# Splitting the head-group results into operand pairs where they are made, instead of in front of the output projection

## The chip, the core and the metric

One core of a Trainium2 chip runs the kernel. The metric is device microseconds of one execution. Three runs of the kernel before gave 2999.87, 3000.15 and 3003.53 us; the median is 3000.15. The profile is of a further execution, which took 2992.77 us.

## What is computed

One decoder layer over 2048 tokens of width 1024, in fp32. The part that the change touches:

```
u = rmsnorm(h, attn_pre_norm)
hq, hf, hi, hg, sq, sk, sv = split(u @ w_in)
o_hg = hgrn2_mix(hq, hf, hi, lb)                       # gated linear recurrence, 4 heads of 128
o_hg = rmsnorm(o_hg, hg_out_norm) * silu(hg)
o_sb = stick_breaking_mix(sq, sk, sv)                  # causal attention, 8 heads of 64
o_sb = rmsnorm(o_sb, sb_out_norm)
mix  = concat(o_hg, o_sb) @ w_out
h    = h + rmsnorm(mix, attn_post_norm)                # then a SwiGLU FFN and a gated embedding
```

The two norms of the group results are by row, so the kernel multiplies the finished product rows by them; it only needs each group's sum of squares per row. The gain `hg_out_norm` is already in the gate; the gain `sb_out_norm` (`g_sb`) has to be put onto the attention result before the product.

## The kernel before

Every fp32 product is made of three fp32r matmuls (`mm3`, lines 215 to 217): each operand is a pair, `hi` (a rounded copy, written by ScalarE) and `lo` (the rest, written by VectorE or GpSimd). Tokens are worked in four groups of 512 (`g` = 0 to 3). A result tile has 128 partitions (columns of the model) by 512 tokens; a group has eight of them for the output projection, 0 to 3 from the recurrence, 4 to 7 from the attention (two heads of 64 in each).

The order of TensorE's instructions is the order in which the program is written: the function `weave` steps a main stream (an input projection, later an output projection) and takes steps of the attention and of the recurrence between its steps. On the other engines and on the DMA queue (SP) a scheduler chooses the order at build time. Every engine then works in order: an instruction that waits holds up all that stand behind it on its engine.

The attention is a chain of 320 units (a block of 128 queries against a chunk of 512 keys). Each unit makes scores (`z`, line 418), weights on ScalarE, VectorE and GpSimd (lines 424 to 443), and four units later transposes them (`turn_of`, `tr`, line 451) and multiplies them with the values (`values_of`, `av`, lines 467 and 468). When the last chunk of a head is done, lines 471 to 474 add the two halves of `av` (a ScalarE copy, a VectorE add) into a tile of 64 partitions, `avo`, and store it in DRAM (`o_s`). The last heads of the groups 0 to 3 end at 206, 462, 796 and 1334 us of the profile. The recurrence (`hgrn`) ends a head with lines 596 to 608: square, gate, store of `gate` to `o_s`; its sum of squares goes through a matmul with ones, line 613, after one further yield.

`out_load(g)` (line 619 on) reads the eight tiles of a group back through a tile `tmp` with two buffers. Of a recurrence tile it makes the pair with a ScalarE cast and a GpSimd subtraction (lines 201, 202); of an attention tile it makes the scaled pair (ScalarE line 629, VectorE line 630), and the square and its sum (ScalarE lines 634, 636, GpSimd line 637). The operands go to `uh` and `ul`, which have 16 pairs of buffers, shared with the operands of the input projection. It is called for group 0 before the last part of the input projection of group 3, and for the groups 1 to 3 before the output projections of the groups 0 to 2, a whole projection before the operands are used. `out_proj(g)` begins with `sums`: four matmuls of `acc` with ones (line 649), two VectorE copies, and two small GpSimd instructions that make the row scales `rg`.

Of the kernel before, what the change touches and what calls it, by code (L numbers as in the profile page):

```python
# [8 lines left out]
F32 = mybir.dt.float32  # L9
F32R = mybir.dt.float32r  # L10
# [80 lines left out]
def hybrid_block(  # L91
# [29 lines left out]
    h2t_s = scratch("h2t_s", (ND, P, GT))  # L121
    pt_s = scratch("pt_s", (PLE // P, P, GT))
    hid_s = [dram.tile([DFF // 256, 7, P, GT], F32, tag=f"hid_s{i}", name=f"hid_s{i}") for i in range(2)]
    o_s = [[dram.tile([P, GT], F32, tag=f"o_s{g}_{i}", name=f"o_s{g}_{i}") for i in range(ND)] for g in range(NG)]


    const = ctx.enter_context(tc.tile_pool(name="const", bufs=1))
# [3 lines left out]
    def ctile(name, shape, dt=F32, pool=const):  # L131
        return pool.tile(list(shape), dt, tag=name, name=name)
# [22 lines left out]
    oml = ctile("oml", (P, HH))  # L155

    masks = {h: ctile(f"mask{h}", (P, BL), U8, const1) for h in (0,) + LEVELS if h < BL}
    hgss = ctile("hgss", (P, NG, TT))


    ps = ctx.enter_context(tc.tile_pool(name="ps", bufs=1, space=bass.MemoryType.PSUM))
# [3 lines left out]
    def bank(tag):  # L165
        return ps.tile([P, 512], F32, tag=tag, name=tag, bufs=BANKS[tag])
# [12 lines left out]
    def ev(dt=F32, name="ev", shape=(P, GT)):  # L179
        return fb.tile(list(shape), dt, tag="ev", name=name, bufs=12)  # L180
# [98 lines left out]
    def operand(pool, tag, bufs):  # L279
        return [pool.tile([P, GT], F32R, tag=tag + s, name=tag + s, bufs=bufs) for s in ("h", "l")]  # L280

    def tmp(dt=F32):
        return wpool.tile([P, GT], dt, tag="tmp", name="tmp", bufs=2)


    def in_norm(g):
# [106 lines left out]
    def attention():  # L393
# [65 lines left out]
        def values_of(ch, sb, lo_c, hi, lo):  # L459
            st, c = ch["st"], ch["c"]  # L460
            g = st["g"]
            first = c == g and sb == 0
            last = c == 0 and sb == TT - 1
            if first:
                st["av"] = bank("av")
            av = st["av"]
            nc.tensor.matmul(av[:, lo_c:], ch["v"][:, sb, :], hi[:, lo_c:], start=first, stop=False)
            nc.tensor.matmul(av[:, lo_c:], ch["v"][:, sb, :], lo[:, lo_c:], start=False, stop=last)
            if last:
                h = st["h"]  # L470
                o = att.tile([SBD, GT], F32, tag="avo", name="avo", bufs=1)
                nc.scalar.copy(o, av[SBD:P, :])
                nc.vector.tensor_tensor(o, av[0:SBD, :], o, op=ALU.add)
                nc.sync.dma_start(o_s[g][HH + h // 2][(h % 2) * SBD:(h % 2 + 1) * SBD, :], o)

        units, turned = [], []
        chunks = [(g, h, c) for g in range(NG) for h in range(SBH) for c in range(g, -1, -1)]
        n_units = len(chunks) * TT
# [22 lines left out]
    def hgrn(g):  # L501
        acc = None
        for h in range(HH):
# [100 lines left out]
                nc.scalar.activation(q.rearrange(flat), ob, AF.Square)  # L604
                nc.gpsimd.tensor_tensor(acc, acc, q, op=ALU.add)
            nc.vector.tensor_tensor(gate.rearrange(flat), ob, gate.rearrange(flat), op=ALU.mult)
            nc.sync.dma_start(o_s[g][h], gate.rearrange(flat))
            nc.gpsimd.tensor_copy(hstate[h], s_last)
            yield
        yield  # L610
        b = bank("hg")
        for c in range(TT):
            nc.tensor.matmul(b[:, c:c + 1], acc[:, c, :], ones1, start=True, stop=True)
        nc.scalar.copy(hgss[:, g, :], b[:, 0:TT])
        yield

    HG_STEPS = HH * 11 + 2


    def out_load(g, res):  # L620
        ops = []
        acc = None
        for i in range(ND):
            raw = tmp()
            nc.sync.dma_start(raw, o_s[g][i])
            if i >= HH:
                hi, lo = operand(wpool, "u", UB)
                gs = g_sb[:, i - HH:i - HH + 1]
                nc.scalar.activation(hi, raw, AF.Copy, scale=gs)
                nc.vector.scalar_tensor_tensor(lo, raw, gs, hi.bitcast(F32), op0=ALU.mult, op1=ALU.subtract)  # L630
                ops.append((hi, lo))
                if i == HH:
                    acc = ev(name="oss")
                    nc.scalar.activation(acc, raw, AF.Square)
                else:
                    nc.scalar.activation(raw, raw, AF.Square)
                    nc.gpsimd.tensor_tensor(acc, acc, raw, op=ALU.add)
            else:
                ops.append(split(wpool, "u", UB, raw))
        res["o"], res["oss"] = ops, acc  # L640

    def out_proj(g, res):
        ops, acc = res["o"], res["oss"]
        r_hg, r_sb = [], []

        def sums(acc):
            b = bank("tr")
            for t in range(TT):
                nc.tensor.matmul(b[:, t:t + 1], acc[:, t * P:(t + 1) * P], ones1, start=True, stop=True)
            rr = const.tile([P, 2 * TT], F32, tag="rg", name="rg", bufs=2)  # L650
            nc.vector.tensor_copy(rr[:, 0:TT], hgss[:, g, :])
            nc.vector.tensor_copy(rr[:, TT:], b[:, 0:TT])
            nc.gpsimd.tensor_scalar(rr, rr, 1.0 / (HH * P), EPS, op0=ALU.mult, op1=ALU.add)
            nc.gpsimd.tensor_tensor(rr, rr, neghalf.to_broadcast((P, 2 * TT)), op=ALU.pow)
            r_hg.extend(rr[:, t:t + 1] for t in range(TT))
            r_sb.extend(rr[:, TT + t:TT + t + 1] for t in range(TT))

        sums(acc)
        mix = [[None, None] for _ in range(TT)]
        for quarter in range(4):  # L660
            half, o = divmod(quarter, 2)
# [708 lines left out]
```

## Time and profile before

| | us |
|---|---|
| median of three runs | 3000.15 |
| profiled execution | 2992.77 |
| its span, first to last instruction | 2990.8 |
| TensorE busy | 2901.4 |
| VectorE busy | 2071.8 |
| ScalarE busy | 1581.7 |
| GpSimd busy | 1398.8 |
| instructions on `tmp`, first start to last end | 918 to 1359, in four sets |

In the views, PE is TensorE, DVE is VectorE, ACT is ScalarE, POOL is GpSimd. A row of the timeline gives start, duration, engine, line, operation, output and input tile, and in brackets how long the engine had been idle and what ended that. A row of the waits gives who waited for whom, the sum in us, how often, and the longest. A row of the windows gives, for a stretch of the span, its length, the busy time of the engines, the granted TensorE clock as a share, and the DMA share and rate.

The sets of `tmp` lie at 918 to 951 (group 0), 1112 to 1151 (group 1), 1214 to 1245 (group 2) and 1320 to 1359 (group 3).

### The profile page before, as it was taken

Reading aid. Unit: us, or ns where it says so; the run is one execution under the profiler, and the core shown is the slowest. Engines: PE = TensorE matmul, PEld = TensorE weight load, DVE = VectorE, ACT = ScalarE, POOL = GpSimd, SP = SyncE. Lnnn points to the kernel's source line nnn. Section 1 sums busy time; section 2 is a strip of 40 time slices with the busy share of each in tenths; the row PEclk is TensorE's granted clock in tenths of the full one; section 3 lists DMA queues with packets and bytes.
Section 4 is the critical chain, followed back from the end, with each engine's and each line's share of the span. In section 5 each row is a group of like instructions: output and inputs, shape, how many; then the busy total and the mean of one; then the engine's idle time right before and its main releaser. Section 6 shows DMA issues by size and latency. Waiting matters only on the chain.

```text
span 2990.8 us, 52665 instructions
## 1 busy us (share of the span) xinstructions
PE 2901.4 (97%) x18188; PEld 2421.3 (81%) x18188; DVE 2071.8 (69%) x2993; ACT 1581.7 (53%) x3182; POOL 1398.8 (47%) x1396
## 2 busy tenths in 40 slices
PE   8999999999999999898999999999999999999999
PEld 7888788878787888788777788888788888878777
DVE  3566667787777776766888777565877765656785
ACT  5666756676667666777523334455433323545542
POOL 3344455555556665865622211355622121456653
PEclk9999999999999999899999999999999999999999
DMA  7775665455445444458877777666965555677974
GB/s 225 210 221 157 182 186 164 141 176 165 145 140 159 144 133 137 160 193 271 278 231 244 246 254 258 196 210 208 344 198 164 164 176 176 208 219 232 327 250 161
DMA packets 469418, 602.26 MB, mean 201 GB/s; under 512 B 43168, under 2 KB 277664, under 8 KB 469152
## 3 DMA queue, kind: packets, MB, share of 16 engines
q1 hardware_dynamic: 469152, 598.91, 63.4%
q8 instruction: 143, 2.34, 0.3%
q14 instruction: 123, 1.01, 0.1%
HBM read 439.89 MB, written 158.86 MB: 200 GB/s over the span
## 4 chain that ended last, share of the span: by engine, by line
PE 46%; DMA 4%; DVE 4%; POOL 3%; issue 2%; ACT 1%; SPq 0%; POOLq 0%; DVEq 0%; ACTq 0%
PE mm L215 6%; PE mm L217 6%; PE mm L216 6%; PE z L217 4%; PE z L215 4%; PE z L216 4%; PE av L216 2%; PE av L217 2%; PE tr L217 2%; PE av L215 2%; PE tr L215 2%; PE tr L216 2%; DVE wl L821 1%; DVE wr L825 1%; DMA wr<-in_w_gate_up_dram 1%
## 5 line engine op out<-in xcount | busy, mean ns | idle before, releaser
L820 ACT CAST wh<-wr 128x512 fp32r<-128x512 f32 x600 | 351.5, 618 | 471.0 <-PE mm L216 195.1
L821 POOL TENSOR_TENSOR wl<-wr,wh 128x512 fp32r<-128x512 f32 x256 | 369.5, 1449 | 469.6 <-ACT wh L820 453.6
L443 POOL TENSOR_TENSOR a<-be,ring 128x512 f32<-128x512 f32 (+2 forms) x320 | 320.4, 1002 | 417.3 <-DVE ring L439 389.2
L215 PE MATMUL mm<-uh,wh 128*128 128x512 f32 x1168 | 480.1, 411 | 5.5 <-DVE vv L358 2.0
L216 PE MATMUL mm<-ul,wh 128*128 128x512 f32 x1168 | 458.3, 392 | 4.0 <-DVE ul L821 2.3
L217 PE MATMUL mm<-uh,wl 128*128 128x512 f32 x1168 | 459.9, 394 | 0.0
L821 DVE TENSOR_TENSOR wl<-wr,wh 128x512 fp32r<-128x512 f32 x344 | 295.9, 867 | 179.0 <-ACT wh L820 156.8
L439 DVE TENSOR_TENSOR_SCAN ring<-z,ring,be 128x512 f32<-128x512 f32 x192 | 245.6, 1279 | 106.2 <-ACT z L425 103.2
L215 PE MATMUL mm<-wh,uh 128*128 128x256 f32 (+1 forms) x992 | 306.0, 309 | 0.0
L216 PE MATMUL mm<-wl,uh 128*128 128x256 f32 (+1 forms) x992 | 292.4, 295 | 0.7 <-POOL wl L821 0.7
L217 PE MATMUL mm<-wh,ul 128*128 128x256 f32 (+1 forms) x992 | 292.5, 295 | 0.0
L217 PEld LDWEIGHTS mm<-uh,wl 128*128 128x128 f32 x1168 | 219.8, 188 | 50.5
L215 PEld LDWEIGHTS mm<-uh,wh 128*128 128x128 f32 x1168 | 220.5, 189 | 49.1 <-issue 2.2
L216 PEld LDWEIGHTS mm<-ul,wh 128*128 128x128 f32 x1168 | 220.9, 189 | 44.8 <-DVE ul L821 2.7
L201 ACT CAST wh<-wr 128x512 fp32r<-128x512 f32 x288 | 178.3, 620 | 120.2 <-PE mm L216 65.8
L202 POOL TENSOR_TENSOR wl<-wr,wh 128x512 fp32r<-128x512 f32 x144 | 189.9, 1318 | 96.4 <-ACT wh L201 90.8
L424 ACT ACTIVATE be<-z 128x512 f32<-128x512 f32 (+2 forms) x320 | 171.0, 534 | 114.6 <-DVE z L422 65.7
L456 DVE TENSOR_TENSOR al<-tr,ah 128x512 fp32r<-128x512 f32 (+1 forms) x320 | 191.8, 599 | 51.0 <-ACT ah L454 49.3
L454 ACT CAST ah<-tr 128x512 fp32r<-128x512 f32 (+1 forms) x320 | 167.7, 524 | 88.0 <-PE tr L451 85.3
L821 POOL TENSOR_TENSOR wl<-s,wh 128x512 fp32r<-128x512 f32 x44 | 69.4, 1580 | 288.7 <-ACT wh L820 241.6
L215 PEld LDWEIGHTS mm<-wh,uh 128*128 128x128 f32 x992 | 190.0, 192 | 8.1
L216 PEld LDWEIGHTS mm<-wl,uh 128*128 128x128 f32 x992 | 190.5, 192 | 6.5 <-POOL wl L821 1.1
(315 smaller groups left out, 7195.4 us busy)
## 6 DMA issues: line engine op xcount, KB each, us to landing
wr<-in_w_gate_up_dram SPq DMA_DIRECT2D x308, 256.0 KB, 4.0
wr<-in_w_in_dram SPq DMA_DIRECT2D x224, 256.0 KB, 3.2
wr<-hid_s SPq DMA_DIRECT2D x154, 256.0 KB, 2.9
wr<-in_w_down_dram SPq DMA_DIRECT2D x110, 256.0 KB, 3.3
wr<-wd_s SPq DMA_DIRECT2D x88, 256.0 KB, 3.2
kt<-k_s SPq DMA_DIRECT2D x80, 256.0 KB, 3.1
vt<-v_s SPq DMA_DIRECT2D x80, 256.0 KB, 3.3
wr<-h_s SPq DMA_DIRECT2D x80, 256.0 KB, 4.2
```

The lines of the kernel that those rows point to most:

```text
L201: nc.scalar.copy(hi, src)
L202: (lo_engine or nc.gpsimd).tensor_tensor(lo, src, hi.bitcast(F32), op=ALU.subtract)
L215: nc.tensor.matmul(o, l[0], r[0], start=start, stop=False)
L216: nc.tensor.matmul(o, l[0], r[1], start=False, stop=False)
L217: nc.tensor.matmul(o, l[1], r[0], start=False, stop=stop)
L424: nc.scalar.activation(be[:, :n], z[:, :n], AF.Sigmoid, scale=0.125)
L439: nc.vector.tensor_tensor_scan(r[:, o:o + n][:, ::-1], z[:, :n][:, ::-1], be[:, :n][:, ::-1], init, op0=ALU.mult, op1=ALU.bypass)
L443: nc.gpsimd.tensor_tensor(a[:, :n], be[:, :n], r[:, o + 1:o + n + 1], op=ALU.mult)
L454: nc.scalar.copy(hi[:, lo_c:], tr[:, lo_c:])
L456: nc.vector.tensor_tensor(lo[:, lo_c:], tr[:, lo_c:], hi[:, lo_c:].bitcast(F32), op=ALU.subtract)
L820: nc.scalar.copy(hi, src)
L821: lo_engine.tensor_tensor(lo, src, hi.bitcast(F32), op=ALU.subtract)
```

## The change

A function `result` makes the pair where a result is finished and stores both tiles; `o_s` has two tiles for each result. `out_load` only loads `uh` and `ul`. The tile `tmp` is gone; `oh` (one buffer, used by recurrence and attention alike) holds `hi` until it is stored, `lo` overwrites the result. `avo` now has 128 partitions and collects two heads; after the second one it is squared, scaled and split. The sum of squares over the four attention tiles is kept in `sbacc`; after the last head of a group four matmuls with ones follow the last value matmul directly, with no yield between them, and ScalarE copies the sums to `oss`. The squares take a buffer of `be`, the tile of the attention weights, which has two.

```
+    def result(g, i, o, gain, lo_engine):
+        hi = wpool.tile([P, GT], F32R, tag="oh", name="oh", bufs=1)
+        lo = o.bitcast(F32R)
+        if gain is None:
+            nc.scalar.copy(hi, o)
+            lo_engine.tensor_tensor(lo, o, hi.bitcast(F32), op=ALU.subtract)
+        else:
+            nc.scalar.activation(hi, o, AF.Copy, scale=gain)
+            lo_engine.scalar_tensor_tensor(lo, o, gain, hi.bitcast(F32), op0=ALU.mult, op1=ALU.subtract)
+        nc.sync.dma_start(o_s[g][i][0], hi.bitcast(F32))
+        nc.sync.dma_start(o_s[g][i][1], o)
...
-                o = att.tile([SBD, GT], F32, tag="avo", name="avo", bufs=1)
-                nc.scalar.copy(o, av[SBD:P, :])
-                nc.vector.tensor_tensor(o, av[0:SBD, :], o, op=ALU.add)
-                nc.sync.dma_start(o_s[g][HH + h // 2][(h % 2) * SBD:(h % 2 + 1) * SBD, :], o)
+                mine, other = slice(h % 2 * SBD, (h % 2 + 1) * SBD), slice((1 - h % 2) * SBD, (2 - h % 2) * SBD)
+                if h % 2 == 0:
+                    avo[0] = att.tile([P, GT], F32, tag="avo", name="avo", bufs=1)
+                o = avo[0]
+                nc.scalar.copy(o[mine, :], av[other, :])
+                nc.vector.tensor_tensor(o[mine, :], av[mine, :], o[mine, :], op=ALU.add)
+                if h % 2:
+                    sq = sb_acc if h == 1 else att.tile([P, GT], F32, tag="be", name="sq")
+                    nc.scalar.activation(sq, o, AF.Square)
+                    if h > 1:
+                        nc.gpsimd.tensor_tensor(sb_acc, sb_acc, sq, op=ALU.add)
+                    result(g, HH + h // 2, o, g_sb[:, h // 2:h // 2 + 1], nc.vector)
+                    if h == SBH - 1:
+                        b = bank("tr")
+                        for t in range(TT):
+                            nc.tensor.matmul(b[:, t:t + 1], sb_acc[:, t * P:(t + 1) * P], ones1, start=True, stop=True)
+                        nc.scalar.copy(oss[:, g, TT:], b[:, 0:TT])
...
-            nc.sync.dma_start(o_s[g][h], gate.rearrange(flat))
+            result(g, h, gate.rearrange(flat), None, nc.gpsimd)
...
     def out_load(g, res):
...
+        res["o"] = [operand(wpool, "u", UB) for _ in range(ND)]
+        for i, pair in enumerate(res["o"]):
+            for n, t in enumerate(pair):
+                nc.sync.dma_start(t.bitcast(F32), o_s[g][i][n])
...
     def out_proj(g, res):
...
-        sums(acc)
+        ops = res["o"]
+        rr = const.tile([P, 2 * TT], F32, tag="rg", name="rg", bufs=2)
+        nc.gpsimd.tensor_scalar(rr, oss[:, g, :], 1.0 / (HH * P), EPS, op0=ALU.mult, op1=ALU.add)
+        nc.gpsimd.tensor_tensor(rr, rr, neghalf.to_broadcast((P, 2 * TT)), op=ALU.pow)
+        r_hg, r_sb = ([rr[:, i * TT + t:i * TT + t + 1] for t in range(TT)] for i in range(2))
```

Where it moves instructions. TensorE at the end of the last attention head of group 0 (206 us in the profile): `av` is the value product, `tr` the transposes of the next unit, `mm` the input projection. Before:

```order
L418 MATMUL z<-kt,q_2577 128x512
L418 MATMUL z<-kt,q_2580 128x512
L467 MATMUL av<-ah,vt 128x128
L468 MATMUL av<-al,vt 128x128
L451 MATMUL tr<-ident,a 128x128 x4
L215 MATMUL mm<-uh,wh 128x512
```

With the change:

```order
L429 MATMUL z<-kt,q_2623 128x512
L429 MATMUL z<-kt,q_2626 128x512
L478 MATMUL av<-ah,vt 128x128
L479 MATMUL av<-al,vt 128x128
L497 MATMUL tr<-ones_193,sbacc 128x1 x4
L462 MATMUL tr<-ident,a 128x128 x4
L216 MATMUL mm<-uh,wh 128x512
```

The four matmuls on `sbacc` stand right behind the last `av`; the transposes and the input projection stand behind them. The same is found at the end of the groups 1, 2 and 3, and the four matmuls on `oss` at the head of each output projection are gone.

GpSimd at the same place; `a` are attention weights, `wl` the low half of a weight tile, `pd` a tile of the recurrence. Before:

```order
L202 TENSOR_TENSOR wl<-wr,wh 128x512
L443 TENSOR_TENSOR a<-be,ring_193 128x512
L443 TENSOR_TENSOR a<-be,ring_195 128x512
L443 TENSOR_TENSOR a<-be,ring_197 128x512
L515 TENSOR_SCALAR pd<-pd,oml,lb 128x512
```

With the change:

```order
L203 TENSOR_TENSOR wl<-wr,wh 128x512
L454 TENSOR_TENSOR a<-be,ring_225 128x512
L492 TENSOR_TENSOR sbacc<-sbacc,sq 128x512
L454 TENSOR_TENSOR a<-be,ring_227 128x512
L541 TENSOR_SCALAR pd<-pd,oml,lb 128x512
```

The addition for the last head stands behind one `a` of the next group.

VectorE where the output projection of group 0 goes over into that of group 1 (1224 to 1232 us); `al` is the low half of the transposed attention weights, `mix` and `h` belong to the norm behind the output projection. Before:

```order
L439 SCALAR_TENSOR_TENSOR ring_197<-z,be 128x384
L706 SCALAR_TENSOR_TENSOR mix<-mix,rstd_16692,gb 128x512 x2
L630 SCALAR_TENSOR_TENSOR ul<-tmp,g_sb,uh 128x512
L707 TENSOR_TENSOR h<-h,mix 128x512
L682 SCALAR_TENSOR_TENSOR mix<-mm,rg,mix 128x256 x2
L422 TENSOR_TENSOR z<-z,maskneg 128x128
L456 TENSOR_TENSOR al<-tr,ah 128x512
```

With the change:

```order
L450 SCALAR_TENSOR_TENSOR ring_229<-z,be 128x384
L705 SCALAR_TENSOR_TENSOR mix<-mix,rstd_16787,gb 128x512 x2
L619 SCALAR_TENSOR_TENSOR sl<-st,tree,hg 128x128
L706 TENSOR_TENSOR h<-h,mix 128x512
L467 TENSOR_TENSOR al<-tr,ah 128x512
L681 SCALAR_TENSOR_TENSOR mix<-mm,rg,mix 128x256 x2
L433 TENSOR_TENSOR z<-z,maskneg 128x128
```

The subtractions for `ul` are gone from here, and `al` stands directly behind the first `h`, ahead of `mix` and `z`.

More of the change, by code (lines that the diff above doesn't have):

```diff
@@ L123, in hybrid_block @@
     hid_s = [dram.tile([DFF // 256, 7, P, GT], F32, tag=f"hid_s{i}", name=f"hid_s{i}") for i in range(2)]
-    o_s = [[dram.tile([P, GT], F32, tag=f"o_s{g}_{i}", name=f"o_s{g}_{i}") for i in range(ND)] for g in range(NG)]
+    o_s = [[[dram.tile([P, GT], F32, tag=f"o_s{g}_{i}_{n}", name=f"o_s{g}_{i}_{n}") for n in range(2)]
+            for i in range(ND)] for g in range(NG)]
     const = ctx.enter_context(tc.tile_pool(name="const", bufs=1))
@@ L157, in hybrid_block @@
     masks = {h: ctile(f"mask{h}", (P, BL), U8, const1) for h in (0,) + LEVELS if h < BL}
-    hgss = ctile("hgss", (P, NG, TT))
+    oss = ctile("oss", (P, NG, 2 * TT))
     ps = ctx.enter_context(tc.tile_pool(name="ps", bufs=1, space=bass.MemoryType.PSUM))
@@ L280, in operand @@
         return [pool.tile([P, GT], F32R, tag=tag + s, name=tag + s, bufs=bufs) for s in ("h", "l")]
-    def tmp(dt=F32):
-        return wpool.tile([P, GT], dt, tag="tmp", name="tmp", bufs=2)
+    def result(g, i, o, gain, lo_engine):
[9 more added lines that the diff above has]
+        nc.sync.dma_start(o_s[g][i][1], o)
     def in_norm(g):
@@ L470, in values_of @@
                 h = st["h"]
-                o = att.tile([SBD, GT], F32, tag="avo", name="avo", bufs=1)
-                nc.scalar.copy(o, av[SBD:P, :])
-                nc.vector.tensor_tensor(o, av[0:SBD, :], o, op=ALU.add)
-                nc.sync.dma_start(o_s[g][HH + h // 2][(h % 2) * SBD:(h % 2 + 1) * SBD, :], o)
+                mine, other = slice(h % 2 * SBD, (h % 2 + 1) * SBD), slice((1 - h % 2) * SBD, (2 - h % 2) * SBD)
[15 more added lines that the diff above has]
+                        nc.scalar.copy(oss[:, g, TT:], b[:, 0:TT])
+        sb_acc = att.tile([P, GT], F32, tag="sbacc", name="sbacc", bufs=1)
+        avo = [None]
         units, turned = [], []
@@ L613, in hgrn @@
             nc.tensor.matmul(b[:, c:c + 1], acc[:, c, :], ones1, start=True, stop=True)
-        nc.scalar.copy(hgss[:, g, :], b[:, 0:TT])
+        nc.scalar.copy(oss[:, g, 0:TT], b[:, 0:TT])
         yield
@@ L620, in out_load @@
     def out_load(g, res):
[L621 to L639, printed above, removed]
@@ L640, in out_load @@
-        res["o"], res["oss"] = ops, acc
-    def out_proj(g, res):
[L643 to L656, printed above, removed]
-        sums(acc)
+        res["o"] = [operand(wpool, "u", UB) for _ in range(ND)]
```

## The prediction

> **What bounds the kernel now.** I read the page first, then the windows, then TensorE's waits in the four stretches in which `out_load` works. The page gives the span and TensorE's share of it:
>
> ```profile
> span 2990.8 us, 52665 instructions
> PE 2901.4 (97%) x18188; PEld 2421.3 (81%) x18188; DVE 2071.8 (69%) x2993; ACT 1581.7 (53%) x3182; POOL 1398.8 (47%) x1396
> ```
>
> TensorE is idle for 89 us in all. Whatever the change does to the time, it does by making that idle time longer or shorter, or by changing the clock. The windows of 100 us (length, busy time of PE, PEld, DVE, ACT and POOL, granted clock, DMA share, GB/s) tell where the idle time lies:
>
> ```profile
> 400.00:500.00 100.00, 99.95 (x960) 85.57 (x960) 70.06 (x116) 62.15 (x137) 54.84 (x69) 1.00 0.56 171
> 1200.00:1300.00 100.00, 89.36 (x1049) 79.96 (x1052) 76.06 (x118) 71.74 (x161) 77.94 (x90) 0.91 0.53 175
> 1300.00:1400.00 100.00, 89.81 (x808) 86.39 (x795) 62.47 (x90) 66.18 (x144) 59.02 (x57) 0.97 0.67 224
> ```
>
> In the attention stretch TensorE leaves nothing over: there a pause of TensorE costs its full length. From 1200 to 1400 it is idle for 21 us and its clock falls below 1. TensorE's waits in the four `out_load` stretches, in this order: 915 to 965, 1110 to 1150, 1200 to 1270, 1330 to 1375 (who waited for whom: us in total, times, longest):
>
> ```profile
> PE av L468 <- DVE al L456: 1.3, 2, 0.8
> PE hg L533 <- POOL qp L570: 0.8, 1, 0.8
> ...
> PE av L467 <- ACT ah L454: 1.7, 1, 1.7
> PE hg L613 <- POOL acc L605: 1.3, 1, 1.3
> PE av L468 <- DVE al L456: 1.3, 2, 0.9
> ...
> PE av L468 <- DVE al L456: 5.4, 2, 4.1
> PE hg L533 <- POOL qp L570: 3.4, 3, 1.7
> PE av L467 <- ACT ah L454: 1.0, 2, 0.5
> ...
> PE z L216 <- POOL wl L202: 8.3, 4, 4.0
> PE z L215 <- ACT wh L201: 0.5, 1, 0.5
> ```
>
> The sums are 2.1, 4.3, 9.8 and 8.8 us: 25 us is the most that can be won in waits. A pause also costs clock. The clock behind the 4.1 us pause, in a stretch with hardly a pause, and behind the 4.0 us pause (length, PE busy, clock, DMA):
>
> ```profile
> 1229.00:1233.00 4.00, 0.18 (x1) 0.75 0.68 228
> 1233.00:1236.00 3.00, 3.00 (x14) 0.50 0.69 223
> 1236.00:1239.00 3.00, 3.00 (x20) 0.69 0.36 109
> 1251.00:1254.00 3.00, 2.36 (x12) 0.58 0.37 121
> 1350.00:1354.00 4.00, 4.00 (x19) 0.51 1.01 340
> ```
>
> After 4.1 us of waiting TensorE worked 3 us at 0.50 and 3 us at 0.69, which is 3 x 0.50 + 3 x 0.31 = 2.4 us lost; after 4.0 us it lost 4 x 0.49 = 2.0 us. So a pause of four microseconds costs about six.
>
> **The change part by part.** What it takes out of the `out_load` stretches, by the rows of `tmp` (count, then shortest, median and longest ns):
>
> ```profile
> L202 POOL TENSOR_TENSOR ul<-tmp,uh x16: 1270/1287/1581, 918.6 to 1334.6; 128x512 fp32r<-128x512 f32 x16
> L629 ACT ACTIVATE uh<-tmp,g_sb x16: 703/723/726, 929.8 to 1351.2; 128x512 fp32r<-128x512 f32 x16
> L630 DVE SCALAR_TENSOR_TENSOR ul<-tmp,g_sb,uh x16: 720/752/1884, 930.6 to 1354.6; 128x512 fp32r<-128x512 f32 x16
> L636 ACT ACTIVATE tmp<-tmp x12: 612/632/639, 934.4 to 1356.7; 128x512 f32<-128x512 f32 x12
> L637 POOL TENSOR_TENSOR oss<-oss,tmp x12: 1277/1297/1739, 937.6 to 1357.4; 128x512 f32<-128x512 f32 x12
> ```
>
> A stretch has 4 of L202, L629 and L630 and 3 of L637: GpSimd loses 4 x 1.29 + 3 x 1.30 = 9.0 us, VectorE 4 x 0.75 = 3.0 us, ScalarE about 8 casts and squares more. None of it is saved: every one of these instructions comes back where a result is made. So the change can only win the waits above, and only in part, since recurrence and norm stay in these stretches.
>
> What it adds to TensorE's path is new. The four matmuls on `sbacc` stand right behind the last `av` of a group, and TensorE can issue nothing behind them until the sum is complete: ScalarE copy, VectorE add, ScalarE square, GpSimd add. Behind them stand the transposes, the scores and the main stream's matmuls. The rows at the ends of the groups 0, 1, 2 and 3, from the timeline (start, duration, engine, line, operation):
>
> ```profile
> 205.64 0.28 PE L468 MATMUL av<-al,vt 128*128 128x128 f32 x1
> 206.95 0.58 ACT L472 COPY avo<-av 64x512 f32<-64x512 f32 x1
> 208.16 0.66 DVE L473 TENSOR_TENSOR avo<-av,avo 64x512 f32<-64x512 f32 x1
> 208.32 1.10 POOL L443 TENSOR_TENSOR a<-be,ring 128x512 f32<-128x512 f32 x1 [0.79 <-DVE ring L439]
> ...
> 461.79 0.40 PE L468 MATMUL av<-al,vt 128*128 128x512 f32 x1
> 463.40 0.68 DVE L473 TENSOR_TENSOR avo<-av,avo 64x512 f32<-64x512 f32 x1 [1.00 <-ACT avo L472]
> 464.81 0.77 POOL L515 TENSOR_SCALAR pd<-pd,oml,lb 128x512 f32<-128x512 f32 x1
> ...
> 795.11 0.39 PE L468 MATMUL av<-al,vt 128*128 128x512 f32 x1
> 796.26 1.09 POOL L443 TENSOR_TENSOR a<-be,ring 128x512 f32<-128x512 f32 x1 [0.65 <-DVE ring L439]
> 796.31 0.68 DVE L473 TENSOR_TENSOR avo<-av,avo 64x512 f32<-64x512 f32 x1
> ...
> 1333.44 0.39 PE L468 MATMUL av<-al,vt 128*128 128x512 f32 x1
> 1334.35 0.68 DVE L707 TENSOR_TENSOR h<-h,mix 128x512 f32<-128x512 f32 x1
> ```
>
> Group 0: the last `av` ends at 205.92, the add at 208.82; a square (0.63) ends at 209.45, when the `a` that stands ahead on GpSimd is also done (209.42); an addition (1.30) ends at 210.75: a pause of 4.8 us. Group 1: 462.19, add 464.08, square 464.7; GpSimd has `pd` ahead until 465.58, the addition ends at 466.9: 4.7 us. Group 2: 795.50, add 796.99, square 797.6, addition 798.9: 3.4 us. Group 3: 1333.83, VectorE busy with `h` until 1335.03, add to 1335.7, square 1336.3, addition 1337.6: 3.8 us. No pause can be shorter than the bare chain, 0.58 + 0.66 + 0.63 + 1.30 = 3.2 us.
>
> - Groups 0 to 2, in stretches where TensorE is full: 4.8 + 4.7 + 3.4 = 12.9 us. The next transposes use the same PSUM bank and wait until ScalarE has copied the sums; between nothing and the 0.58 of the copy above I take 0.3 each, 0.9 in all. The clock: 2.2 for each of the two long pauses, between the 2.0 and 2.4 above, and 1.7 for the short one, an estimate between the 1.3 lost in the row at 1251 (3 x 0.42) and 2.0; 6.1 together. That is 19.9. While TensorE pauses, the other engines work ahead, and I let two later waits of the 0.8 to 0.9 us kind go: **+18**. Ends: 3 x 3.2 without any clock less 2, which is 8, and 12.9 + 0.9 + 3 x 2.4, which is 21.
> - Group 3 falls into the last stretch. Now it is 8.8 us of waits and 2.0 of clock, 10.8. Then: a pause of 3.8 and its 2.0, and I leave 2.5 of the waits for `wl`, since GpSimd is rid of 9.0 us of work and catches up in the pause. 8.3 against 10.8: **-2.5**. Ends: -5 if no wait is left, +2 if most are.
> - The stretch 1200 to 1270: 9.8 us of waits, 2.4 of clock at 1233 and 3 x 0.42 = 1.3 at 1251, 13.5. Ahead of the `al` that ends the 4.1 us pause two L630 are gone (1.5 us), and `mix` and `z` now stand behind it. GpSimd loses 9.0 and gets one split of a recurrence head (1.3). But the norm's instructions on VectorE and GpSimd stay. I take half: **-7**. Ends: -12 and -2.
> - The stretch 1110 to 1150: 4.3 us, behind casts of `uh` and additions of `oss` in part: **-3**, ends -4.3 and 0. The stretch at 915: **-1**, ends -2 and 0.
> - The same instructions, spread over the attention: 16 times L202 and 12 times L637 on GpSimd, 16 of L630 on VectorE, and their ScalarE partners. What hides them is that a unit's weights are made four units ahead of their transposes; the row at 400 shows GpSimd at 55% and TensorE with 0.05 us idle, with the recurrence running. Exposed in full they would be 16 x 1.29 + 12 x 1.30 = 36 us on GpSimd alone; I take **+2.5**, near the lower end of nothing, and 6 as the upper end in the range.
> - `oh` and `avo` have one buffer, so a second result waits until the first is stored. The DMA rows at `o_s`, and the one close pair, an attention store and the square of a recurrence head:
>
> ```profile
> DMA to landing us min/median/max: 2.0/2.9/5.5
> ...
> 910.10 0.47 SPq L474 DMA_DIRECT2D o_s<-avo  x1
> 911.57 0.60 ACT L604 ACTIVATE q<-hg 128x512 f32<-128x512 f32 x1 [0.37 <-PE hg L598]
> ```
>
> A store issued at 910.10 or a little later lands at 913 to 914; the recurrence wants `oh` near 912.9. ScalarE would stand for a microsecond, with sigmoids and `ah` behind it, inside the lead of four units: nothing here, and part of the 6 above.
> - DMA: 64 loads of 0.26 MB in place of 32, and 8.4 MB more stores. SP issues 16 loads in a row now, and each waits until TensorE has released the operand's buffer, with weight and key loads queued behind. Before, SP stood at the same place for a free `tmp`. At a DMA share of 0.53 to 0.67 in these stretches I cost it at nothing; without that cover it would be a landing, 2.9 us, for each of the four calls.
> - The tiny VectorE copies and the row scales leave the head of the projections: nothing.
>
> The sum: 18 - 2.5 - 7 - 3 - 1 + 2.5 = **+7 us**. Against the profiled execution's own 2992.8 that is 2999.8; the median of three is 7.4 us above the profiled execution, so as a median it is 3000.15 + 7 = 3007 us. What a measurement of this kernel can tell from no change is about 0.2%, or 6 us.
>
> [...]
>
> **The rivals.**
> - *The relief is larger than the pauses.* For it: 25 us of waits and over 5 us of lost clock sit in the stretches that are relieved, and most are ended by an engine that loses work. Then the terms are 13 (pauses near 3.3 us, 1.6 of clock each, less 2), -5, -12, -4, -2 and 0: -10, **2990 us**. It decides if the new pauses stay under about 3.5 us each and the 4.1 us pause falls below 2. Against it: three of the four pauses come out above 3.4 with the queues as they are.
> - *The two cancel*, each a little on the good side: **3001 us**. For it: pauses and relief are of one size, and TensorE does the same work.
> [...]
> - *The single buffers stall ScalarE.* If a dozen of the 32 results find `oh` or `avo` not yet stored and TensorE loses 1 us each: 7 + 12, **3019 us**. Against it: the results lie far apart but for close pairs like that at 910.
>
> **How the numbers follow.** The forecast, 3007, has 0.36 and the stalled ScalarE 0.06: slower 0.42. Cancelling 0.21 and the clock 0.08: within 0.2%, 0.29. The larger relief: faster 0.29. With all lower ends the sum is 8 - 5 - 12 - 4.3 - 2 + 0 = -15, with all upper ends 21 + 2 - 2 + 0 + 0 + 6 = +27. All ends together are unlikely; the range takes -12 to +21, which is 2988 to 3021, and holds the rivals' times. For the forecast alone it would be 3006 to 3018.
>
> **What would show it.** In the profile after: TensorE's waits should have a new row, the matmul on `sbacc` waiting for GpSimd's addition, four times, 16 to 17 us in total, with the clock below 1 behind each. The 4.1 us pause near 1230 should be below 2.5, and the waits for `wl` after 1338 below 4 in sum. The prediction is wrong if the row on `sbacc` sums to less than 11 us, if the clock stays at 1 behind the pauses, or if the waits from 1100 to 1400 fall by more than 18 us.

## The result, and the profile after

The changed kernel takes 3019.3 us (median of 6 runs) against 2999.6 of the kernel before: a ratio of 1.0075, 95% interval [1.0063, 1.0087]. That is 20 us slower by the medians and 22 by the ratio. The forecast was 7 us slower. The profiled execution took 3018.84 us, 26.1 more than that of before. First the page of the changed kernel, then two of its largest waits over the whole span, and last the row of the kernel before that answers to the second:

```profile
span 3017.1 us, 52727 instructions
PE 2906.5 (96%) x18188; PEld 2427.5 (80%) x18188; DVE 2066.9 (69%) x2985; ACT 1581.6 (52%) x3186; POOL 1403.9 (47%) x1396
```

```profile
PE tr L497 <- POOL sbacc L492: 19.0, 4, 5.2
PE z L217 <- POOL wl L203: 9.1, 5, 3.4
```

```profile
PE z L216 <- POOL wl L202: 9.4, 6, 4.0
```

No engine's busy time differs from that of before by more than 5.1 us. TensorE is idle for 111 us instead of 89, and the new row on `sbacc`, four waits, is 19 of it. The waits for `wl` have not become less. Two windows that answer to those of before:

```profile
400.00:500.00 100.00, 94.62 (x937) 81.38 (x936) 65.89 (x106) 57.81 (x124) 57.42 (x72) 0.97 0.59 175
1300.00:1400.00 100.00, 88.34 (x846) 83.62 (x845) 53.37 (x85) 64.10 (x136) 58.56 (x61) 0.93 0.81 279
```

From 400 to 500 TensorE was idle for 0.05 us before and is for 5.4 now. In the window from 1300 to 1400 VectorE has 53 us of work where it had 62, TensorE has not gained, and the clock is lower. (The changed kernel reaches the same work 16 to 25 us later, so the windows answer to each other only roughly.) The four pauses in TensorE's timeline, then the clock around the first of them (length, PE, PEld, DVE, ACT, POOL, clock, DMA):

```profile
212.10 1.87 PE L497 MATMUL tr<-ones,sbacc 128*128 128x1 f32 x8 [5.17 <-POOL sbacc L492]
...
477.49 1.87 PE L497 MATMUL tr<-ones,sbacc 128*128 128x1 f32 x8 [5.13 <-POOL sbacc L492]
...
821.23 1.87 PE L497 MATMUL tr<-ones,sbacc 128*128 128x1 f32 x8 [3.60 <-POOL sbacc L492]
...
1354.81 1.87 PE L497 MATMUL tr<-ones,sbacc 128*128 128x1 f32 x8 [5.05 <-POOL sbacc L492]
```

```profile
207.00:212.10 5.10, 0.00 (x0) 0.00 (x0) 2.73 (x3) 2.76 (x5) 3.84 (x4) 0.81 0.37 104
212.10:214.10 2.00, 1.87 (x8) 1.78 (x8) 0.50 (x1) 0.09 (x1) 0.00 (x0) 0.50 0.66 252
214.10:217.00 2.90, 2.78 (x9) 2.39 (x10) 0.69 (x1) 0.66 (x2) 0.00 (x0) 0.51 0.02 7
```

The same behind the shortest pause, that of group 2:

```profile
821.20:824.00 2.80, 2.52 (x11) 2.44 (x12) 0.53 (x1) 0.16 (x1) 0.00 (x0) 0.50 0.87 321
824.00:827.00 3.00, 3.00 (x40) 2.22 (x39) 1.22 (x3) 1.50 (x5) 0.64 (x1) 0.50 0.00 1
827.00:830.00 3.00, 3.00 (x14) 2.43 (x13) 1.02 (x2) 2.75 (x6) 0.00 (x0) 0.84 0.17 61
```

At a clock of 0.50 the matmuls of the input projection start 0.43 us apart (215.56 and 215.99), at 1.00 they start 0.23 apart (205.67 and 205.90), so I count half of the work at half clock as lost. 4.9 us of work behind the first pause ran at half clock, 2.4 us lost; behind the shortest it is 1.4 + 1.5 + 0.5 = 3.4. Group 1, read in the same way, lost 2.9.

To see where the time went I took each matmul's start in both timelines (the n-th with the same operands) and the difference. Since TensorE's work is nearly the same, a step in it is time won or lost at that place. Median over the 25 us that begin at the place, in us, the place by the span of before; the last columns belong to experiments below, `before_again` being a second profile of the kernel before. Every column comes from one profile:

| at | changed | late_sums | keep_warm40 | late_norm | before_again |
|---|---|---|---|---|---|
| 175 | 1.0 | 1.8 | 1.4 | 2.3 | 3.6 |
| 225 (group 0 ended) | 9.5 | 3.5 | 9.4 | 3.8 | 3.9 |
| 425 | 10.2 | 5.0 | 11.3 | 4.8 | 3.9 |
| 500 (group 1 ended) | 19.3 | 7.9 | 19.5 | 7.8 | 3.9 |
| 775 | 22.1 | 10.8 | 22.4 | 10.6 | 3.7 |
| 825 (group 2 ended) | 29.1 | 14.7 | 27.6 | 12.9 | 3.6 |
| 975 | 27.1 | 12.8 | 25.5 | 11.1 | 4.3 |
| 1100 | 27.4 | 13.1 | 25.9 | 11.5 | 4.3 |
| 1175 | 19.4 | 5.1 | 17.8 | 3.5 | 4.8 |
| 1300 | 16.1 | 2.6 | 16.0 | 0.2 | 6.2 |
| 1425 (group 3 ended) | 25.4 | 6.4 | 22.8 | 1.3 | 7.2 |
| 1525 | 26.7 | 8.2 | 24.1 | 2.4 | 6.4 |
| 1675 | 25.8 | 3.8 | 24.4 | -1.6 | 6.5 |
| 2875 | 25.5 | -1.5 | 20.2 | -3.8 | 5.2 |

Two executions of one program differ at the start (3.6 us) and from 1250 on (2 us), but between 175 and 900 they keep the same distance within 0.3 us: steps of several us there are the change.

Now the places where the change was to win. First TensorE's waits in the relieved stretch (1200 to 1270 before), then in the last one:

```profile
1249.14 0.50 PE L479 MATMUL av<-al,vt 128*128 128x512 f32 x1 [1.81 <-DVE al L467]
...
1281.78 0.37 PE L479 MATMUL av<-al,vt 128*128 128x128 f32 x1 [3.42 <-DVE al L467]
...
1369.79 0.39 PE L217 MATMUL z<-wl,uh 128*128 128x256 f32 x1 [2.56 <-POOL wl L203]
...
1386.42 0.39 PE L217 MATMUL z<-wl,uh 128*128 128x256 f32 x1 [3.37 <-POOL wl L203]
```

The pause of 4.1 us is down to 1.81, but 3.42 us come 33 us later; TensorE's waits of this stretch sum to 8.7 us where they were 9.8. What stood ahead of the `wl` for which TensorE waited at 1386 is no split and no square; GpSimd, and VectorE beside it:

```profile
1378.65 5.27 POOL L706 TENSOR_TENSOR h<-h,mix 128x512 f32<-128x512 f32 x1 [2.30 <-DVE mix L705]
1383.88 1.26 POOL L820 TENSOR_TENSOR wl<-wr,wh 128x512 fp32r<-128x512 f32 x1
1385.10 1.26 POOL L203 TENSOR_TENSOR wl<-wr,wh 128x512 fp32r<-128x512 f32 x1
```

```profile
1379.69 0.68 DVE L706 TENSOR_TENSOR h<-h,mix 128x512 f32<-128x512 f32 x1
1380.30 0.68 DVE L203 TENSOR_TENSOR wl<-wr,wh 128x512 fp32r<-128x512 f32 x1
1380.90 1.89 DVE L820 TENSOR_TENSOR ul<-wr,uh 128x512 fp32r<-128x512 f32 x3
```

It is an addition of the norm, which the change left where it was; its twelve instances (shortest, median, longest ns):

```profile
L706 POOL TENSOR_TENSOR h<-h,mix x12: 1265/1663/5267, 1247.9 to 1447.6; 128x512 f32<-128x512 f32 x12
```

The chain of group 3's own sum met the norm too. Its ScalarE copy ended at 1350.56, and VectorE then had an `h` ahead of the addition:

```profile
1350.27 1.75 DVE L706 TENSOR_TENSOR h<-h,mix 128x512 f32<-128x512 f32 x1
...
1352.05 0.69 DVE L487 TENSOR_TENSOR avo<-av,avo 64x512 f32<-64x512 f32 x1
```

One relieved stretch did better than forecast. The window at 1100, before and then changed (where the same work lies some 27 us later):

```profile
1100.00:1200.00 100.00, 92.66 (x944) 78.84 (x942) 67.81 (x105) 63.93 (x135) 63.39 (x79) 0.97 0.43 131
```

```profile
1100.00:1200.00 100.00, 96.31 (x995) 82.22 (x995) 73.25 (x111) 66.52 (x145) 62.65 (x77) 1.00 0.57 177
```

TensorE works 3.7 us more in it, all at full clock, where it had lost 3 us of clock.

The last stretch, 1300 to 1525 of the span of before, with the end of group 3's attention, for the kernel before, the changed kernel and `late_sums` (the first experiment below), each from its own start to its own end of the same work:

```profile
1300.00:1525.00 225.00, 205.07 (x1482) 186.78 (x1469) 156.08 (x220) 134.60 (x285) 123.78 (x107) 0.98 0.74 247
```

```profile
1316.10:1551.70 235.60, 209.18 (x1471) 190.50 (x1458) 146.72 (x217) 130.54 (x277) 116.55 (x100) 0.96 0.74 252
```

```profile
1302.60:1533.20 230.60, 210.45 (x1474) 192.18 (x1461) 149.15 (x215) 129.41 (x277) 112.21 (x100) 0.96 0.76 256
```

TensorE is idle for 19.9, 26.4 and 20.2 us in them. The clock's records stand at half for 6.8, 17.1 and 20.5 us, and half of TensorE's busy time under them is lost: 2.0, 7.9 and 9.4 us.

### The profile page after: what moved, and what is told of

It reads as the page before. It is cut to its first block, busy times and chain, and to the rows that moved or that the text cites. A ratio compares the mean times of both kernels' runs of the same rounds, so it can differ in the third digit from the quotient of the medians.

```text
span 3017.1 us, 52727 instructions
## 1 busy us (share of the span) xinstructions
PE 2906.5 (96%) x18188; PEld 2427.5 (80%) x18188; DVE 2066.9 (69%) x2985; ACT 1581.6 (52%) x3186; POOL 1403.9 (47%) x1396
```

## The experiments

Each ratio is to runs of the kernel before on the same chip, with its 95% interval. The experiments ran on four chips: `late_sums`, `stall_only`, `hg_only` and `wide_bufs` on one, `late_sums012`, `keep_warm`, `one_load` and `late_wide` on a second, `keep_warm40`, `late1` and `late_norm` on a third, `before_norm` and `after_norm` on a fourth. Two ratios from different chips are compared only through the kernel before, and no experiment was run on two of the chips.

| kernel | ratio | interval |
|---|---|---|
| changed | 1.0075 | [1.0063, 1.0087] |
| late_sums | 0.9987 | [0.9977, 0.9997] |
| stall_only | 1.0117 | [1.0102, 1.0132] |
| late_sums012 | 1.0021 | [1.0010, 1.0031] |
| late1 | 1.0029 | [1.0020, 1.0039] |
| keep_warm (13) | 1.0079 | [1.0066, 1.0091] |
| keep_warm40 | 1.0050 | [1.0031, 1.0070] |
| hg_only | 0.9987 | [0.9978, 0.9997] |
| wide_bufs | 1.0052 | [1.0037, 1.0067] |
| late_wide | 1.0009 | [0.9999, 1.0020] |
| one_load | 1.0004 | [0.9995, 1.0014] |
| late_norm | 0.9961 | [0.9946, 0.9976] |
| before_norm | 0.9979 | [0.9969, 0.9989] |
| after_norm | 1.0052 | [1.0036, 1.0068] |

**Without the pauses, and with nothing but the pauses.** `late_sums` is the changed kernel with the sums issued later:

```
-                    if h == SBH - 1:
-                        (four matmuls on sb_acc, copy to oss)
+                    if h == SBH - 1 and g < NG - 1:
+                        pending.append([4, g])        # issued four units later, ahead of turn_of
...
     def out_proj(g, res):
+        if g == NG - 1:
+            sb_sums(g)                                # the same four matmuls and copy
```

> The changed kernel, with the four matmuls that sum the attention's squares issued later: four attention units later for the groups 0 to 2, at the head of the output projection for group 3. All else of the change stays. Theory (TensorE stands at the sums, and each stand with the clock behind it costs 7 to 9 us): the three steps of 8.4, 9.3 and 7.0 us at the group ends go, and 4 to 6 us of the stretch after 1340, so 28 to 31 us below the changed kernel, which is 2988 to 2992 us and 8 to 12 below the kernel before; no row with a wait on sbacc of over 1 us. Rival (the loss comes from the same vector and scalar work spread over the attention, the pauses only show it): at most 8 us below the changed kernel, 3011 us or more.

It measured 0.9987, so 0.88% or 26 us less than the changed kernel, a little short of the theory's 28 to 31; the profiled execution is 27.3 us shorter (2991.51). No row of its waits is on `sbacc`. TensorE's timeline at the sum of group 1 shows no wait in front of the sums:

```profile
480.96 1.00 PE L409 MATMUL tr<-ones,sbacc 128*128 128x1 f32 x8
482.21 0.66 PE L470 MATMUL tr<-ident,a 128*128 128x128 f32 x4 [0.25 <-ACT oss L410]
```

So the loss hangs on where four matmuls stand: the rival's 8 us at most are ruled out. The steps in the table say where. At the ends of the groups 0 to 2 they fall from 8.5, 9.1 and 7.0 to 1.7, 2.9 and 3.9 us, which is 16.1, and in the stretch from 1300 to 1525 from 10.6 to 5.6. They do not go altogether: the sums still take 1.00 us, and 0.25 us more until the next transposes have their bank, pause or not, and one half clock stands at 815. By 1525 the two profiles are 18.5 us apart. The other 8.5 us come behind it, where neither kernel has sums: there the changed kernel's clock stood at half for 6.8 us each at 1698 and 2156, which cost 6.0 us of work, and that of `late_sums` not at all. That this part comes from the pauses is not shown.

`stall_only` is the other half, the kernel before with a pause of the same kind, the square, the addition and the sums that make it, and nothing else of the change:

```
+                if h == SBH - 1:
+                    sq = att.tile([P, GT], F32, tag="be", name="sq")[0:SBD, :]
+                    nc.scalar.activation(sq, o, AF.Square)
+                    nc.gpsimd.tensor_tensor(sq, sq, o, op=ALU.add)
+                    (four matmuls of sq with ones into bank "tr", ScalarE copy to probed)
```

> The kernel before, and only a pause added: behind the last attention head of each group ScalarE squares its result, GpSimd adds, four matmuls sum it and ScalarE copies the sums to a tile that nobody reads (extra work, the result is unused). Theory: four pauses of 3 to 5 us with the clock behind them, 6 to 8 us each, of which the fourth is partly covered: 20 to 30 us above the kernel before, 3020 to 3030. Rival (the other engines work ahead in a pause and later waits go): under 8 us above.

```profile
PE tr L481 <- POOL sq L478: 21.1, 4, 7.9
```

1.0117, 35 us: more than expected. The steps in its timeline at the four group ends are 8.6, 9.6, 6.6 and 10 us, together 35. The pause of group 3, of which I had let a part be covered, cost most: GpSimd was late there, and the wait 7.9 us.

**The pause of group 3 alone.** `late_sums012` moves the sums of the groups 0 to 2 and leaves those of group 3:

> The changed kernel, with the four summing matmuls issued four attention units later for the groups 0 to 2 only; group 3 keeps its sums right behind its last attention head. Against the kernel with all four moved (ratio to the kernel before 0.9987) this tells what the pause of group 3 costs. Theory (that pause too is paid in full, 5.0 us and the clock behind it, as the steps of the trace suggest): 5 to 9 us above that kernel, a ratio of 1.0004 to 1.002. Rival (the last stretch waits for weights anyway and covers it, as the prediction had it): within 2 us of that kernel, a ratio of 0.998 to 0.9995.

1.0021 against 0.9987: about 10 us (0.34%) for this one pause, a little above the theory's 5 to 9, but from two chips. By the steps from 1300 to 1525 it is 6.2 us (11.8 against 5.6), and the rest comes behind the stretch. Either way the waits for weights cover little of it: those for `wl` sum to 8.2 us with the pause and 7.7 without it.

**What of a pause is clock.** `keep_warm` puts work of no use ahead of the sums, so that TensorE doesn't stand idle:

```
                         b = bank("tr")
+                        for t in range(13):
+                            nc.tensor.transpose(b[:, t % TT * P:(t % TT + 1) * P], ident, ident)
```

> The changed kernel, with 13 transposes of the identity (0.27 us each, 3.5 us, results unused) ahead of each of the four sums, so that TensorE works through most of each pause. The sums come at the same time as before; only the clock behind the pauses can differ. In the changed kernel's records the clock stands at half for 6.83 us at each of the four pauses, of which 4.9, 5.8 and 6.8 us lie on work in the groups 0 to 2: 2.4 + 2.9 + 3.4 = 8.7 us, and about 3 in group 3. Theory (a third of the cost of a pause is the clock): 8 to 12 us below the changed kernel, a ratio of 1.0035 to 1.005, and no half clock behind the sums. Rival (the clock falls anyway, or the cost behind a pause is something else): within 3 us of the changed kernel, 1.0065 or more.

```profile
207.81 1.61 PE L497 MATMUL tr<-ident 128*128 128x128 f32 x13
...
213.14 1.86 PE L499 MATMUL tr<-ones,sbacc 128*128 128x1 f32 x8 [3.73 <-POOL sbacc L492]
```

1.0079, nothing won, but the run does not decide: one transpose has 0.27 us in its row (the median of those on L462 in the changed kernel), but 13 in succession took 1.61 us, not 3.5. TensorE still idled for 3.73 us, and the sums still took 1.86 (half clock). So again with 40:

> As the run with 13 transposes ahead of each sum, now with 40. In that run the 13 took 1.61 us together (0.12 each, they overlap), left 3.73 us idle, and the clock fell for 6.83 us as before; 40 take about 4.8, so that TensorE hardly idles at the sums of the groups 0, 1 and 3 and overshoots by about 1.2 us in group 2. Theory (the clock is a third of the cost): no half clock behind the sums, and 6 to 11 us below the changed kernel, a ratio of 1.004 to 1.0055. Rival (the clock behind a pause isn't what costs): 1.0065 or more, even where the clock stays at 1.

First the timeline, then the windows (length, PE, PEld, DVE, ACT, POOL, clock, DMA):

```profile
207.22 4.55 PE L497 MATMUL tr<-ident 128*128 128x128 f32 x40
212.56 1.05 PE L499 MATMUL tr<-ones,sbacc 128*128 128x1 f32 x8 [0.79 <-POOL sbacc L492]
```

```profile
211.00:212.00 1.00, 0.77 (x8) 0.53 (x5) 0.20 (x1) 0.77 (x2) 0.77 (x1) 1.00 0.19 65
212.00:213.00 1.00, 0.44 (x4) 0.45 (x5) 1.00 (x1) 0.00 (x0) 0.50 (x1) 1.00 0.37 141
213.00:214.00 1.00, 0.75 (x7) 0.66 (x7) 0.05 (x1) 0.16 (x1) 0.00 (x0) 1.00 0.39 148
214.00:215.00 1.00, 1.00 (x6) 0.91 (x6) 0.00 (x0) 0.44 (x1) 0.00 (x0) 0.69 0.60 236
```

1.0050 against 1.0075, about 7.5 us less, within the theory's range; but the intervals overlap, and `wide_bufs` below came as low without touching the clock. The sums are back at 1.05 us. The half clock is gone behind the sums of the groups 2 and 3 and half as long behind the other two. In the table of steps the three group ends are 8.0, 8.2 and 5.2 us instead of 8.5, 9.1 and 7.0, and the stretch from 1300 to 1525 is 8.1 instead of 10.6: 5.7 of 35 us came back. By the changed kernel's own windows the clock is 8.7 of the 24.6 us at the three group ends, about a third; of that the dummy transposes win back 3.2, and behind two of the three sums the clock still falls. The rest is the wait, which the dummy work did not shorten (at group 0 the sums begin 5.45 us after the last `av`, 5.44 in the changed kernel), and the sums.

**How far away is far enough.** `late1` is `late_sums012` with `pending.append([1, g])`:

> The changed kernel, with the sums of the groups 0 to 2 issued one attention unit later instead of four; group 3 as in the changed kernel. The kernel with four units had 1.0021. Theory (a unit lasts longer than the chain of 3.6 to 5.2 us, or nearly): waits on sbacc of under 1.5 us each in these groups, and within 4 us of the kernel with four units, 1.001 to 1.0035. Rival (one unit is less than the chain): waits of 2 us and more remain, with half a clock behind them, 1.004 to 1.006.

```profile
PE tr L503 <- POOL sbacc L492: 8.3, 4, 5.0
```

5.0 of the 8.3 us are group 3's, so 1.1 us on average are left at the others, and the time is 1.0029 against 1.0021. One unit hides most of the chain.

**A second profile of the kernel before.**

> The kernel before, unchanged, for a second profile of it: how far two executions of one program differ stretch by stretch. Theory (a step of a few us in one profile can be scatter): steps of 1 to 4 us at the start and in the last 1400 us, none above 1 us between 100 and 1300. Rival (executions of one program agree): no step above 1 us.

Its column stands in the table above: the start moves it by 3.6 us and the stretch around 1275 by 1.5. The theory holds, but for that last step.

**Other reasons that were open.** `hg_only` is the kernel before with the recurrence's results alone split where they are made, pair loads for these four operands, and one buffer for `tmp`:

> The kernel before, with the recurrence's half of the change alone: its results are split where they are made and loaded as pairs; the attention's results still come through tmp (which has one buffer instead of two, for room). No sum is moved. Theory (the stretches that load are relieved by the splits that leave them): 4 to 8 us below the kernel before, at 1100 to 1270 us of the span. Rival (the relief is in the attention's half and the norm, and the pair loads cost as much): within 3 us of the kernel before or slower.

0.9987, about 4 us, at the lower end. In its timeline the stretch at 1110 wins 5.3 us, and that from 1300 to 1525 loses 3.1. `wide_bufs` gives the results more buffers (`hi = ev(F32R, "oh")`, and `bufs=2` for `avo`); `late_wide` is the same on top of `late_sums`:

> The changed kernel, with twelve buffers instead of one for the split results (oh) and two for the attention's pairs (avo). Theory: nobody waits long for these buffers, within 4 us of the changed kernel. Rival (single buffers stall ScalarE, and TensorE behind it): 8 to 15 us below the changed kernel, 3004 to 3011 us.

> The kernel with all four sums moved, and twelve buffers for the split results, two for the attention's pairs. The buffers alone gave about 6 us on the changed kernel (1.0052 against 1.0075, intervals that just overlap). Theory (they are worth that much, and the two edits add): a ratio of 0.9965 to 0.9975. Rival (that gain was the scatter of the runs, or came only beside the pauses): 0.998 to 0.999.

1.0052 alone, 0.23% or 7 us less than the changed kernel, between what the theory and its rival had, with intervals that overlap. Its three group ends still cost 9.0, 9.0 and 6.9 us. Beside `late_sums`, at 0.9987, `late_wide` has 1.0009, 0.22% more, and fits neither expectation. So the single buffers are not what costs 20 us; that they cost nothing is not shown. `one_load` is `late_sums` with a pair in one tile, loaded by one transfer:

```
+        boths = [wpool.tile([P, 2 * GT], F32R, tag="u", name="u", bufs=UB) for _ in range(ND)]
...
+            nc.sync.dma_start(b.bitcast(F32).rearrange("p (n t) -> p n t", n=2), o_s[g][i].rearrange("n p t -> p n t"))
```

> The kernel with all four sums moved (ratio 0.9987), where each pair also lies in one tile and is loaded by one transfer of 0.5 MB: 8 loads per group from SyncE's queue, as many as the kernel before has, not 16. Theory (what the last stretch still loses comes from SyncE's queue, in which weight loads stand behind 16 loads): 3 to 8 us below that kernel, a ratio of 0.996 to 0.9977. Rival (the number of loads doesn't matter, the bytes or nothing at all do): within 2 us of it.

1.0004: no gain over the whole, against the theory. But that does not clear the transfers in the last stretch: in the one profile of `one_load` the stretch from 1300 to 1525 wins 1.5 us where `late_sums` loses 5.6, and in that of `late_wide` it loses 0.9. The kernels with late sums differ there by 7 us in their profiles, and lose or win it again elsewhere. What makes them differ is open.

**The norm's additions.** `late_norm` is `late_sums` with one more line changed, `before_norm` and `after_norm` have that line alone:

```
-                (nc.gpsimd if j else nc.vector).tensor_tensor(hs[j], hs[j], d, op=ALU.add)
+                nc.vector.tensor_tensor(hs[j], hs[j], d, op=ALU.add)
```

> The kernel with all four sums moved (0.9987), with both additions of the norm behind the output projection on VectorE, where one of the two was on GpSimd. In the changed kernel one such addition took 5.27 us on GpSimd, ahead of the split for which TensorE waited 3.4 us. Theory (the waits for wl in the last stretch end behind the norm's work on GpSimd, which the change left there): the waits for wl from 1325 on fall by 3 us or more, and 2 to 6 us below that kernel, a ratio of 0.9967 to 0.998. Rival (VectorE is as late as GpSimd was): within 2 us of that kernel or above.

> The kernel before, and only the second addition of the norm moved from GpSimd to VectorE. Theory (the norm's additions on GpSimd bound the waits for wl from 1200 on, and did so before the change): 4 to 9 us below the kernel before, a ratio of 0.997 to 0.9987. Rival (before the change VectorE had 4 splits of 0.75 us per stretch in the same place, and the addition only moves the wait there; the change's relief is what makes it worth something): within 2 us, or above.

> The changed kernel, and only that same edit. Theory: the gain of 4 to 9 us is there too, a ratio of 1.0045 to 1.0062 to the kernel before, since it comes from the norm and has nothing to do with the sums. Rival of the theory (the pause of group 3 gives GpSimd time to finish the norm's additions, so the edit has nothing to win): 1.0065 or more.

0.9961, 0.9979 and 1.0052: the line is worth 0.26% on `late_sums`, 0.21% on the kernel before and 0.23% on the changed one. Only the second is a comparison on one chip with intervals well apart; the three together say that the change's relief is not what makes it worth something. My expectation of where the gain lies did not hold. The waits for `wl` from 1325 to 1530, first in `late_sums`, then in `late_norm`:

```profile
PE z L217 <- POOL wl L203: 5.3, 4, 2.1
...
PE av L217 <- POOL wl L203: 2.4, 2, 1.4
```

```profile
PE av L217 <- POOL wl L203: 4.4, 3, 2.1
PE z L217 <- POOL wl L203: 4.0, 3, 1.7
```

They are 7.7 and 8.4 us: not less. By the steps from 1300 to 1525, `late_norm` loses 2.2 us where `late_sums` loses 5.6, and `after_norm` 6.2 where the changed kernel loses 10.6. (Of the 5.8 us that `late_norm` is ahead at 1525, 1.6 were there at 1175, before the first of these additions.) But `before_norm` loses 1.4 there, and the second profile of the kernel before 0.2: on the kernel before the line relieves nothing in this stretch. What it gains there shows at the head of the FFN, from 1570 to 1750, where TensorE is idle for 5.7 us before, 5.3 in the second profile of the kernel before, and not at all in `before_norm`. In `after_norm` it is idle there for 7.1 us. So the line helps on all three kernels, at different places, and why is open.

The version that beats both kernels is `late_norm`: the change, its sums four units later, the norm's additions on VectorE. It takes 2986.0 us against 2997.1, 1.1% less than the changed kernel by the two ratios. Against `before_norm`, which has the line without the change, it is 0.2% less, with intervals that overlap.

## Why the prediction was right or wrong

The sign and the main mechanism were right: a new wait of TensorE on the sum of squares, at four places, that costs more than the relief brings. The size was about a third of what came. The step that failed most is the term for group 3 and the last stretch, forecast at -2.5 and measured at +10.6; next comes the term for the pauses, 18 instead of 24.6. That 3019.3 us still lies in the stated range is luck: these two terms and that for 1110 came out beyond their own ends (+2, 21 and -4.3), and 1110 gave back 5 us more than forecast. By its own steps, in us:

| step | forecast | measured | from the table of steps |
|---|---|---|---|
| pauses of the groups 0 to 2 | +18 | +24.6 | 8.5 + 9.1 + 7.0 |
| group 3 and the last stretch | -2.5 | +10.6 | 16.1 to 26.7, from 1300 to 1525 |
| stretch at 1200 | -7 | -3.3 | 19.4 to 16.1 |
| stretch at 1110 | -3 | -8.0 | 27.4 to 19.4 |
| stretch at 915 | -1 | -2.0 | 29.1 to 27.1 |
| spread over the attention | +2.5 | +4.5 | 1.0 + 0.7 + 2.8; the first can be scatter |

- **The pauses.** The chain was read rightly from the rows: 13.9 us of waits against 12.9. The clock was mis-sized, 8.7 instead of 6.1: I took the 2.0 to 2.4 us that earlier pauses had cost, and 1.7 for the short one, but the short one cost most, 3.4. And the four matmuls themselves were missing: 1.25 us each time with their hand-over, where I had 0.3. They were in the kernel before too, at the head of the output projection, and took 0.9 us there (1136.05 to 1136.94); that time is gone from the stretches at 1110 and 1200, where I had not counted it either. The three parts make 26.4, and the steps 24.6; the difference fits the 2 us that I let the other engines give back, but no run shows it by itself.
- **Group 3** is the step that failed in sign. "I leave 2.5 of the waits for `wl`, since GpSimd is rid of 9.0 us of work and catches up in the pause." The two long waits for `wl` in this stretch are 5.9 us, besides the pause of 5.05, and over the whole stretch the row is 9.1 us where it was 9.4. So next to nothing of these waits went, although GpSimd's work in the whole stretch fell from 123.8 to 116.6 us. In one place, at 1386, the wait ended behind an addition of the norm, and the sum's own chain waited behind an `h` on VectorE; but `late_norm` takes those additions off GpSimd, and its waits for `wl` are no less. Why GpSimd did not catch up is open. The clock was missed too: I counted 2.0 us, as before, and it was 7.9. `late_sums012` shows that the pause is paid, with 6 us by the steps and 10 by the ratios. Without it, in `late_sums`, the stretch still loses 5.6 us, and that is clock and not waiting: TensorE is idle for 20.2 us, as before (19.9), but the half clock costs 9.4 us instead of 2.0. Why the clock falls more often with no more idle time is open.
- **The stretch at 1200**: the 4.1 us pause fell below 2.5 as forecast, and a new one of 3.4 us came on the same kind of instruction. From 1175 to 1300 of the span of before TensorE was idle for 12.4 us, and is for 13.0 in the same work now; what the stretch won is clock, 3.4 us lost at half instead of 6.9. I had this clock too small: my row at 1251 ends at 1254, but the clock stood at half until 1258.3, which cost 2.6 us and not 1.3.
- **The stretch at 1110**: I counted the waits, 4.3 us, and forgot the clock, although the window of before has it at 0.97. From 1100 to 1175 of the span of before TensorE was idle for 5.5 us, and is for 2.4 in the same work now; the half clock cost 3.4 us there, and costs nothing now.
- **The single buffers** would have given 3019 us, the time that came, by chance: with more of them the kernel was still 0.52% slower than before, and beside late sums more buffers won nothing.
- **The clock.** The half clock covers 4.9, 5.8 and 6.8 us of work behind pauses of 5.2, 5.1 and 3.6 us, so what a pause loses does not follow its length. In the records the clock stands at half for 6.83 us at each of the four pauses of the changed kernel. No run shows it fall at some of these pauses only, the 0.08 of the prediction: it fell at all four, and of the three in the groups 0 to 2 the shortest lost most, 3.4 us. Nor does it take a pause of microseconds: in `keep_warm40` the longest wait ahead of the drop at 214 was 0.79 us, and TensorE was busy for 1.96 of the 3 us ahead of it.

Of the tests that the prediction set itself: `sbacc` 19.0 us instead of 16 to 17, the clock below 1 behind each, the 4.1 us pause at 1.81; the waits for `wl` not below 4, but 9.1.

## What to carry to other kernels

Before a reduction is put behind the last instruction of a full engine, follow the chain that it needs through every other engine: an engine that works in order waits for all of it (here TensorE started nothing from 207.00 to 212.10 us, with the transposes and the input projection behind the sums). Write such consumers some steps later; here one unit took three quarters of the wait of the groups 0 to 2 away (13.9 us to 3.3), four all of it, for a line of code. When work is taken from a queue, do not book the waits on that queue as won: here 7 us of work left GpSimd in the last stretch, and the waits for its `wl` stayed as they were. And price the clock with the waits, from whole records and not from the first microseconds: at 1200 all that was won was clock, and in the last stretch 5.9 us of what was lost.

## What the runs showed of the hardware

- A row's duration is no rate here. One transpose has 0.27 us in its row, 40 in succession took 4.55 in `keep_warm40`, 0.11 each.
- The clock fell without an idle stretch as long as the drop: in `keep_warm40` 0.79 us of waiting and sums of one column each (1.05 us), behind busy work, were followed by 3.4 us at half clock (0.69, 0.50, 0.50 and 0.60 in the four windows from 214 to 218).
- The longest of GpSimd's additions of the norm lies beside a busy VectorE. That of 1378.65 took 5.27 us, four times the shortest (1.27), while VectorE ran without a break until 1382.8; GpSimd's next instruction began only at 1383.88. It is one row, and no run here separates VectorE from other causes.
